# Values and gates of a retention layer as seven half-size products per head in place of eight, with shared sums, in a two-layer trunk on one core

## The chip, the cores and the metric

One Trainium2 chip, one of its cores. The metric is the device time in microseconds of one execution of the program. The engines are called as in the profile: PE does the matmuls (PEld its weight loads), DVE, ACT and POOL do elementwise work, SP issues the loads and stores.

## The reference, cut to what matters

The program is a trunk of two layers over 512 tokens of width 1024. Layer A is a retention layer with 4 heads (keys of 256, values of 512), layer B a latent attention layer with 16 heads. Layer A is what the change touches:

```python
hproj = x @ w_in
qk = H_A * DK_A                                   # 1024
q = hproj[..., :qk].reshape(b, s, H_A, DK_A)
k = hproj[..., qk:2 * qk].reshape(b, s, H_A, DK_A)
v = hproj[..., 2 * qk:2 * qk + WIDTH_A].reshape(b, s, H_A, DV_A)
gate = hproj[..., 2 * qk + WIDTH_A:]
q = _rope(q, ROPE_BASE_A)
k = _rope(k, ROPE_BASE_A) * (DK_A ** -0.5)
o = _chunkwise_retention(q, k, v)                 # decayed causal q k^T v
...
o = ((o - mu) * lax.rsqrt(var + 1e-5)).astype(x.dtype).reshape(b, s, WIDTH_A)
return (o * jax.nn.silu(gate)) @ w_out
...
x = _layer_norm(DEEPNORM_ALPHA * x + y, ln_g[layer], ln_b[layer])
```

For one head, V and the gate are both x (512 x 1024) times a weight of 1024 x 512.

## The kernel before, in words

Every float32 product is made of three matmuls (`mm3`, L84 to L88): each operand is split into a high part, rounded to the format that PE multiplies, and a low part, the rest; high by high, high by low and low by high are summed in PSUM. `split` (L90 to L92) makes the parts: a cast on ACT, then a subtraction on DVE.

The class `Weights` brings the weights in the order of the list `order`: `issue` takes a staging tile (tag `wst`, 2 buffers), starts the load on SP, casts the high part on ACT (L56) and subtracts the low part (L58) on DVE, for every third tile on POOL. `get` keeps two tiles ahead of the one asked for; there are four pairs of high and low parts.

Layer A runs head by head. `proj_qk(h)` makes q and k transposed and applies the rope (L295 to L303) on DVE: two products with an operand in PSUM, a subtraction of two tiles in SBUF, two products, an addition, then the split, for q and for k. `proj_v(h)` and `gate(h)` both call `token_proj` (L309 to L318): four weight tiles, each against four token tiles and two blocks of the contraction, three matmuls of 128x512 each, so 96 a call. Between the two stand the `scores(h)`, which need the rope. `gate` takes tanh on ACT and one operation on DVE. `inner(h)` multiplies the decayed scores by V, one token tile after another, and normalises: statistics (L368, L369) and the argument of the root on DVE, the power on POOL (L202), a product with the gate on DVE (L372), a scaling on ACT (L375). After `inner(h)` comes `out_proj(h - 1)` (96 matmuls into the residual `r`), then `proj_qk(h + 1)`, then `transposes(h)`, 16 transposes of 128x128 and their splits. After the last head, `out_proj(3)` runs token tile by token tile with the layer norm and the transposes of the result.

Layer B begins with the latent projections. The inverse norms of the query latents are four powers on POOL (L202), one per token tile; each lets DVE normalise its tile (L591, L592), which PE then transposes (L242). The rope of the shared key is five operations on POOL (L597 to L601); the rotated key is transposed at L629. `gate_b` (L86 with x1h, then L611 and L613) fills PE ahead of it.

The order on each engine is that of a scheduler, which takes the program's order as priority; each engine's queue is then fixed and runs in order. Loads are issued from SP in program order.

Of the kernel before, what the change touches and what calls it, by code (L numbers as in the profile page):

```python
# [8 lines left out]
F32 = mybir.dt.float32  # L9
# [25 lines left out]
class Weights:  # L35
# [6 lines left out]

    def issue(self, between=None):

        nc = self.nc
        name, aps, n = self.todo.pop(0)
        st = self.stage.tile([P, WC], F32, tag="wst", name="wst")
# [3 lines left out]
        for j, ap in enumerate(aps if isinstance(aps, list) else [aps]):  # L51
# [3 lines left out]
            nc.sync.dma_start(st[:, sl], ap)  # L55
# [15 lines left out]
def trunk_kernel(ctx, tc, a):  # L71
# [106 lines left out]
    zero = keep.tile([P, 512], BF16, tag="kvg", name="zero")  # L178
# [5 lines left out]
    kvg = keep.tile([P, KVL], F32, tag="kvg", name="kvg")  # L184
# [72 lines left out]
    with tc.tile_pool(name="pa", bufs=1) as pa:  # L257
        cosA = pa.tile([P, S], F32, tag="cosA", name="cosA")
        sinA = pa.tile([P, S], F32, tag="sinA", name="sinA")
        decay = pa.tile([P, H_A, S], F32, tag="decay", name="decay")  # L260
# [3 lines left out]
        qk, vv, sT, gs, og, oT = {}, {}, {}, {}, {}, {}  # L264

        def proj_qk(h):
            first = {}
            if h == 0:
                for nm in ("q", "k"):
                    first[nm] = [bank(), bank()]  # L270
                for k in range(KX):
# [5 lines left out]
                    banks = first["q"] + first["k"]  # L277

                    steps = [(i, j) for j in range(3) for i in range(4)] if k == 0 else [(i, j) for i in range(4) for j in range(3)]
                    for i, j in steps:  # L280
                        l, x_ = parts[j]
                        nc.tensor.matmul(banks[i], lhsT=l[:, sls[i]], rhs=x_, start=k == j == 0, stop=k == KX - 1 and j == 2)  # L282
            for nm in ("q", "k"):
                ps = first.get(nm, [])
# [12 lines left out]
                eng = nc.vector
                eng.tensor_tensor(out=rr[:, 0, :], in0=ta, in1=tb, op=ALU.subtract)
                tc_ = pa.tile([P, S], F32, tag="ropeA", name="ropeA")
                td = pa.tile([P, S], F32, tag="ropeB", name="ropeB")  # L300
# [617 lines left out]
```

## Time and profile before

| | |
|---|---|
| median of 3 runs | 947.59 us (947.55 to 949.78) |
| the profiled execution | 947.91 us, span 946.1 us |
| mean granted clock of PE | 0.995 of full |
| busy share of the span | PE 99%, DVE 57%, ACT 35%, POOL 15% |
| layer A, layer B | to about 430 us, from there |

The page gives the busy time of each engine over the span, and the chain of work that ended last. As the engines run side by side, only time on that chain counts: work on DVE, ACT or POOL matters where PE waits for it. A wait shows as the time in brackets behind a row of the timeline, with what ended it, and summed in the view of waits.

### The profile page before, as it was taken

To read this page: it belongs to the slowest core of one execution; us is meant where nothing else is said; L and a number is where in the kernel's file an instruction comes from. 1 tells how busy PE (TensorE), PEld (TensorE's weight loads), DVE (VectorE), ACT (ScalarE), POOL (GpSimd) and SP (SyncE) were. 2 spreads that over 40 slices of the span, in tenths; PEclk is the share of its full clock that TensorE was granted. 3 is DMA by queue.
4 is the path that set the end of the run, shared out by engine and by line. 5 is a ranking of instruction groups with operands and counts; after the bars stand their busy time and mean duration, and the time that the engine had idled before them with its cause. 6 is when DMAs were issued, how large, how long until landed. Compare 5 with 4: busy or idle time off the path is not lost.

```text
span 946.1 us, 11987 instructions
## 1 busy us (share of the span) xinstructions
PE 933.2 (99%) x4649; PEld 792.9 (84%) x4649; DVE 538.9 (57%) x1015; ACT 333.7 (35%) x576; POOL 144.1 (15%) x99
## 2 busy tenths in 40 slices
PE   9999999999999999999989999999999999999996
PEld 6888888888888888888968888888888888888885
DVE  5745545363535435853365667474664737647567
ACT  5333333233323333223433443343343334333431
POOL 0112111111121123012211101001011021111104
PEclk9999999999999999999999999999999999999998
DMA  8832222222212324113224323342233422424222
GB/s 263 294 115 68 89 90 67 89 89 89 89 63 94 106 73 156 45 37 123 62 93 118 113 68 96 105 115 75 78 103 99 111 68 90 117 78 112 90 65 91
DMA packets 31497, 94.30 MB, mean 100 GB/s; under 512 B 4176, under 2 KB 4816, under 8 KB 31440
## 3 DMA queue, kind: packets, MB, share of 16 engines
q1 hardware_dynamic: 27936, 83.96, 27.9%
q10 hardware_dynamic: 3504, 9.57, 4.1%
q8 instruction: 36, 0.59, 0.3%
q14 instruction: 21, 0.17, 0.1%
HBM read 83.03 MB, written 2.10 MB: 90 GB/s over the span
## 4 chain that ended last, share of the span: by engine, by line
PE 93%; issue 3%; DVE 2%; POOL 1%; ACT 0%; DVEq 0%; POOLq 0%; ACTq 0%
PE ps L88 28%; PE ps L87 28%; PE ps L86 28%; PE ps L282 2%; PE ps L678 2%; PE ps L655 1%; PE ps L656 1%; PE ps L386 1%; PE ps L242 1%; PE ps L182 0%; POOL ln_rs L202 0%; POOL rs L202 0%; DVE r L729 0%; POOL wlo L58 0%; DVE wlo L58 0%
## 5 line engine op out<-in xcount | busy, mean ns | idle before, releaser
L56 ACT CAST whi<-wst 128x1024 fp32r<-128x1024 f32 (+3 forms) x159 | 151.4, 953 | 306.5 <-PE ps L88 148.7
L58 POOL TENSOR_TENSOR wlo<-wst,whi 128x1024 fp32r<-128x1024 f32 (+3 forms) x49 | 109.8, 2241 | 682.5 <-ACT whi L56 657.6
L58 DVE TENSOR_TENSOR wlo<-wst,whi 128x1024 fp32r<-128x1024 f32 (+3 forms) x110 | 121.8, 1109 | 150.1 <-ACT whi L56 149.6
L86 PE MATMUL ps<-whi,xTh 128*128 128x512 f32 x256 | 100.1, 391 | 0.0
L87 PE MATMUL ps<-wlo,xTh 128*128 128x512 f32 x256 | 99.6, 389 | 0.0
L88 PE MATMUL ps<-whi,xTl 128*128 128x512 f32 x256 | 99.6, 389 | 0.0
L86 PE MATMUL ps<-qlt_h,whi 128*128 128x512 f32 x144 | 56.9, 395 | 0.0
L663 ACT ACTIVATE p<-ps,sm 128x512 f32<-128x512 f32 (+1 forms) x64 | 33.4, 526 | 66.6 <-DVE sm L660 66.6
L87 PE MATMUL ps<-qlt_l,whi 128*128 128x512 f32 x144 | 56.5, 392 | 0.0
L88 PEld LDWEIGHTS ps<-whi,xTl 128*128 128x128 f32 x256 | 48.1, 188 | 10.0
L88 PE MATMUL ps<-qlt_h,wlo 128*128 128x512 f32 x144 | 56.4, 391 | 0.0
L87 PEld LDWEIGHTS ps<-wlo,xTh 128*128 128x128 f32 x256 | 48.1, 188 | 9.7
L86 PEld LDWEIGHTS ps<-whi,xTh 128*128 128x128 f32 x256 | 48.1, 188 | 9.7
L86 PE MATMUL ps<-x1h,whi 128*128 128x512 f32 x128 | 50.6, 396 | 0.0
L86 PE MATMUL ps<-whi,oTh 128*128 128x512 f32 x128 | 50.0, 391 | 0.0
L87 PE MATMUL ps<-x1l,whi 128*128 128x512 f32 x128 | 50.0, 390 | 0.0
L88 PE MATMUL ps<-x1h,wlo 128*128 128x512 f32 x128 | 49.9, 390 | 0.0
L87 PE MATMUL ps<-wlo,oTh 128*128 128x512 f32 x128 | 49.8, 389 | 0.0
L88 PE MATMUL ps<-whi,oTl 128*128 128x512 f32 x128 | 49.6, 390 | 0.0
L86 PE MATMUL ps<-whi,ogh 128*128 128x512 f32 (+1 forms) x114 | 44.7, 392 | 0.0
L88 PE MATMUL ps<-whi,ogl 128*128 128x512 f32 (+1 forms) x114 | 44.1, 387 | 0.0
L87 PE MATMUL ps<-wlo,ogh 128*128 128x512 f32 (+1 forms) x114 | 44.0, 386 | 0.0
(202 smaller groups left out, 2111.2 us busy)
## 6 DMA issues: line engine op xcount, KB each, us to landing
wst<-in_w_v SPq DMA_DIRECT2D x16, 512.0 KB, 3.3
wst<-in_w_g SPq DMA_DIRECT2D x16, 512.0 KB, 3.3
wst<-in_w_ao SPq DMA_DIRECT2D x16, 512.0 KB, 3.3
wst<-in_w_gb SPq DMA_DIRECT2D x16, 512.0 KB, 3.8
qr<-uv ACTq DMA_DIRECT2D x64, 128.0 KB, 2.4
wst<-in_w_bo SPq DMA_DIRECT2D x16, 512.0 KB, 3.7
wst<-in_w_qk SPq DMA_DIRECT2D x12, 512.0 KB, 3.3
wst<-in_w_q SPq DMA_DIRECT2D x16, 384.0 KB, 3.1
```

What stands on the lines that cost most here:

```text
L56: nc.scalar.copy(hi[:, sl], st[:, sl])
L58: eng.tensor_tensor(out=lo[:, sl], in0=st[:, sl], in1=hi.bitcast(F32)[:, sl], op=ALU.subtract)
L86: nc.tensor.matmul(ps, lhsT=lh, rhs=rh, start=start, stop=False)
L87: nc.tensor.matmul(ps, lhsT=lh, rhs=rl, start=False, stop=False)
L88: nc.tensor.matmul(ps, lhsT=ll, rhs=rh, start=False, stop=stop)
L242: nc.tensor.transpose(out=ps[:, k * P : (k + 1) * P], in_=src[:, k * P : (k + 1) * P], identity=ident)
L282: nc.tensor.matmul(banks[i], lhsT=l[:, sls[i]], rhs=x_, start=k == j == 0, stop=k == KX - 1 and j == 2)
L386: nc.tensor.transpose(out=ps[:, k * P : (k + 1) * P], in_=og[h][:, n, k * P : (k + 1) * P], identity=ident)
L655: nc.tensor.matmul(ps, lhsT=rh[:, qs], rhs=krp[:, :n], start=False, stop=False)
L656: nc.tensor.matmul(ps, lhsT=rl[:, qs], rhs=krp[:, :n], start=False, stop=True)
L663: nc.scalar.activation(pp, ps, AF.Exp, bias=sm[:, qb, 1:2], scale=SCALE_B, accum_out=sm[:, qb, 2:3])
L678: nc.tensor.transpose(out=ps[:, do : do + P], in_=pr[i][:, so : so + P], identity=ident)
```

## The change

With x in four quarters (token halves by halves of the contraction) and the joined weights V|G in four quarters (halves of the contraction by V and gate), the two projections are one 2 x 2 block product. The change computes it with seven products of quarters (`product`, 24 matmuls each) in place of eight, by the scheme of Strassen with shared sums:

- `x_forms` makes four sums of quarters of x once, on POOL, and splits each on ACT and DVE (128x1024).
- `w_vg` brings the four weight quarters of a head, two tiles of 128x1024 each, and makes four sums of quarters: those of `p6` on DVE, those of `p5` and `p7` on POOL, two tiles each. Fourteen weight tiles a head are then split, where there were eight. The first `W.load` of a tile is done in the function that stands in the list; the others reuse what lies in the staging tiles. One quarter is loaded twice.
- `values_and_gates` runs P1, P6, the scores, P2, P5, P7, P4, P3, and adds the products up from PSUM on DVE (`plus`, 14 a head), with two copies on ACT. V is then split, and the gate taken, from tiles in SBUF.
- Staging tiles of layer A: eight in place of two. Layer B has its own two. Tiles share tags in other ways (rope with the scores' parts, q and k with v, the products' sums with the transposed output); the decay is loaded per head; norm weights are loaded later.
- `out_proj(h)` follows `transposes(h)` for heads 0 to 2. Head 3's transposes follow `inner(3)` at once.
- In layer B two of the rope operations on POOL are kept in program order, and the scheduler's order on POOL comes out another way.

The diff, cut to its core:

```diff
+    def w_vg(h):
+        v, g, s = a["w_v"], a["w_g"], {}
+
+        def sub(out, x, y, eng):
+            eng.tensor_tensor(out=out, in0=x, in1=y, op=ALU.subtract)
+            return out
+
+        def p1(t):
+            s["v0", t] = W.load(v[4 * h + t])
+            return s["v0", t]
+
+        def p6(t):
+            s["g0", t] = W.load(g[4 * h + t])
+            s["g1", t] = W.load(g[4 * h + 2 + t])
+            sub(s["v0", t], s["g0", t], s["v0", t], nc.vector)
+            return sub(s["g1", t], s["g1", t], s["v0", t], nc.vector)
+
+        def p2(t):
+            s["v1", t] = W.load(v[4 * h + 2 + t])
+            return s["v1", t]
+
+        def p5(t):
+            sub(s["v1", t], s["v1", t], s["g1", t], nc.gpsimd)
+            return s["v0", t]
+
+        def p7(t):
+            s["g1", t] = W.load(g[4 * h + 2 + t])
+            return sub(s["g0", t], s["g1", t], s["g0", t], nc.gpsimd)
...
     for h in range(H_A):
-        order += w_a("w_v", "v", h) + w_a("w_g", "g", h)
-        if h:
-            order += w_a("w_ao", "o", h - 1)
+        order += w_vg(h)
         if h + 1 < H_A:
             order += [(f"qk{h + 1}", a["w_qk"][4 * h + t], 1024) for t in range(4)]
-    order += w_a("w_ao", "o", H_A - 1)
+        order += w_a("w_ao", "o", h)
...
+        def x_forms():
+            a11, a12 = xv[:, 0:4, 0:256], xv[:, 4:8, 0:256]
+            a21, a22 = xv[:, 0:4, 256:512], xv[:, 4:8, 256:512]
+            f1, f2, f3 = (wst.tile([P, 4, 256], F32, tag="wst", name="xsum") for _ in range(3))
+            nc.gpsimd.tensor_tensor(out=f1, in0=a21, in1=a22, op=ALU.add)
+            nc.gpsimd.tensor_tensor(out=f2, in0=f1, in1=a11, op=ALU.subtract)
+            split(*forms["s2"], f2)
+            nc.gpsimd.tensor_tensor(out=f3, in0=a11, in1=a21, op=ALU.subtract)
+            split(*forms["s3"], f3)
+            split(*forms["s1"], f1)
+            nc.gpsimd.tensor_tensor(out=f2, in0=a12, in1=f2, op=ALU.subtract)
+            split(*forms["s4"], f2)
...
+        def product(name, x_):
+            ps = [bank(), bank()]
+            for t in range(2):
+                wh, wl = W.get(name)
+                for n in range(2):
+                    for j in range(2):
+                        k = 2 * t + j
+                        sl = slice(j * 512, (j + 1) * 512)
+                        mm3(ps[n], x_(k, n), (wh[:, sl], wl[:, sl]), k == 0, k == 3)
+            return ps
+
+        def values_and_gates(h):
...
+            ps1 = product(f"p1.{h}", block(0, 0))
+            for n in range(2):
+                nc.scalar.copy(m[:, 0, n, :], ps1[n])
+            ps6 = product(f"p6.{h}", form("s2"))
+            for n in range(2):
+                plus(m[:, 1, n, :], m[:, 0, n, :], ps6[n])
+            scores(h)
+            ps2 = product(f"p2.{h}", block(4, 0))
...
+            for n in range(2):
+                split(hi[:, n, :], lo[:, n, :], plus(tmp("v"), m[:, 0, n, :], ps2[n]))
+            ps5 = product(f"p5.{h}", form("s1"))
+            for n in range(2):
+                plus(c[:, n, :], m[:, 1, n, :], ps5[n])
+            ps7 = product(f"p7.{h}", form("s3"))
+            for n in range(2):
+                plus(m[:, 0, n, :], m[:, 1, n, :], ps7[n])
+                gated(2 + n, plus(c[:, 2 + n, :], m[:, 0, n, :], ps5[n]))
+            ps4 = product(f"p4.{h}", block(4, 2))
+            for n in range(2):
+                split(hi[:, 2 + n, :], lo[:, 2 + n, :], plus(tmp("v"), m[:, 0, n, :], ps4[n]))
+            ps3 = product(f"p3.{h}", form("s4"))
+            for n in range(2):
+                gated(n, plus(c[:, n, :], c[:, n, :], ps3[n]))
...
         proj_qk(0)
+        x_forms()
         for h in range(H_A):
-            proj_v(h)
...
-            scores(h)
-            gate(h)
+            values_and_gates(h)
...
             inner(h)
-            if h:
-                for half in range(2):
-                    w = [W.get(f"o{h - 1}") for _ in range(2)]
-                    for n in range(NT):
-                        out_proj(h - 1, half, n, w)
             if h + 1 < H_A:
                 proj_qk(h + 1)
             transposes(h)
+            if h + 1 < H_A:
+                for half in range(2):
+                    w = [W.get(f"o{h}") for _ in range(2)]
+                    for n in range(NT):
+                        out_proj(h, half, n, w)
...
-        nc.gpsimd.tensor_tensor(out=ta, in0=raw, in1=cosB, op=ALU.mult)
-        nc.gpsimd.tensor_tensor(out=tb[:, :, 0:32], in0=raw[:, :, 32:64], in1=sinB[:, :, 0:32], op=ALU.mult)
+        tc.keep_in_program_order(nc.gpsimd.tensor_tensor(out=ta, in0=raw, in1=cosB, op=ALU.mult))
+        tc.keep_in_program_order(
+            nc.gpsimd.tensor_tensor(out=tb[:, :, 0:32], in0=raw[:, :, 32:64], in1=sinB[:, :, 0:32], op=ALU.mult)
+        )
```

The order on three queues, in rows of the instruction lists of the two kernels (line, operation, output <- inputs, shape). The first place is DVE after the last split of x, from there to the rope of head 0. Before (`wlo` at L58 are the low parts of weights):

```order
L92 TENSOR_TENSOR xTl<-r,xTh 128x512
L58 TENSOR_TENSOR wlo<-wst,whi 128x512
L58 TENSOR_TENSOR wlo<-wst,whi 128x1024 x2
L295 TENSOR_TENSOR ropeA<-ps,cosA 128x512
L296 TENSOR_TENSOR ropeB<-ps,sinA 128x512
L58 TENSOR_TENSOR wlo<-wst,whi 128x1024
L298 TENSOR_TENSOR rope<-ropeA,ropeB 128x512
```

And now (L65 makes low parts of weights, L100 is `split`, L115 a sum of weights):

```order
L100 TENSOR_TENSOR xTl<-r,xTh 128x512
L65 TENSOR_TENSOR wlo<-wst,whi 128x512
L100 TENSOR_TENSOR s1l<-xsum,s1h 128x1024
L65 TENSOR_TENSOR wlo<-wst,whi 128x1024
L100 TENSOR_TENSOR s2l<-xsum,s2h 128x1024
L65 TENSOR_TENSOR wlo<-wst,whi 128x1024
L100 TENSOR_TENSOR s3l<-xsum,s3h 128x1024
L100 TENSOR_TENSOR s4l<-xsum,s4h 128x1024
L378 TENSOR_TENSOR ropeA<-ps,cosA 128x512
L379 TENSOR_TENSOR ropeB<-ps,sinA 128x512
L382 TENSOR_TENSOR ropeA<-ps,cosA 128x512
L380 TENSOR_TENSOR rope<-ropeA,ropeB 128x512
```

The four forms of x stand ahead of the rope; further down the same queue, the first low part for P6 (the L65 row here) stands behind a sum of weights and most of the rope:

```order
L115 TENSOR_TENSOR wst<-wst 128x1024
L379 TENSOR_TENSOR ropeB<-ps,sinA 128x512
L100 TENSOR_TENSOR qkl<-rope,qkh 128x1024
L380 TENSOR_TENSOR rope<-ropeA,ropeB 128x512
L382 TENSOR_TENSOR ropeA<-ps,cosA 128x512
L383 TENSOR_TENSOR ropeB<-ps,sinA 128x512
L65 TENSOR_TENSOR wlo<-wst,whi 128x1024
L384 TENSOR_TENSOR rope<-ropeA,ropeB 128x512
```

The second place is PE around the end of head 3, before, at the end of `inner(3)`:

```order
L86 MATMUL ps<-vh,sTh 128x512
L87 MATMUL ps<-vl,sTh 128x512
L88 MATMUL ps<-vh,sTl 128x512
L86 MATMUL ps<-whi,oTh 128x512
L87 MATMUL ps<-wlo,oTh 128x512
```

Here the last matmuls of `inner(3)` are followed by the 96 of `out_proj(2)`, and the transposes come after them. Now:

```order
L94 MATMUL ps<-vh,sTh 128x512
L95 MATMUL ps<-vl,sTh 128x512
L96 MATMUL ps<-vh,sTl 128x512
L494 MATMUL ps<-ident,gs 128x128 x16
L94 MATMUL ps<-whi,oTh 128x512
```

The 16 transposes follow `inner(3)` with nothing between. The third place is POOL in layer B, before:

```order
L202 TENSOR_TENSOR rs<-rs_t,mhalf 128x1 x3
L597 TENSOR_TENSOR rbA<-krt,cosB 128x256
L598 TENSOR_TENSOR rbB<-krt,sinB 128x4x32
L599 TENSOR_TENSOR rbB<-krt,sinB 128x4x32
L601 TENSOR_TENSOR krt<-rbA,rbB 128x4x64 x2
L202 TENSOR_TENSOR rs<-rs_t,mhalf 128x1
```

And now:

```order
L250 TENSOR_TENSOR rs<-rs_t,mhalf 128x1 x3
L711 TENSOR_TENSOR rbB<-krt,sinB 128x4x32
L250 TENSOR_TENSOR rs<-rs_t,mhalf 128x1
L707 TENSOR_TENSOR rbA<-krt,cosB 128x256
L709 TENSOR_TENSOR rbB<-krt,sinB 128x4x32
L713 TENSOR_TENSOR krt<-rbA,rbB 128x4x64 x2
```

The fourth power moved from behind the rope of the key to behind its first product.

## Rows read from the trace of the kernel before

**Rows 1.** The page's busy line: us, share of the span, instructions.

```profile
PE 933.2 (99%) x4649; PEld 792.9 (84%) x4649; DVE 538.9 (57%) x1015; ACT 333.7 (35%) x576; POOL 144.1 (15%) x99
```

**Rows 2.** Windows: length, busy PE, PEld, DVE, ACT, POOL; clock, DMA, GB/s.

```profile
103.00:203.00 100.00, 100.00 (x461) 83.47 (x459) 46.96 (x70) 30.46 (x39) 14.19 (x9) 1.00 0.27 87
...
464.00:485.00 21.00, 17.48 (x89) 14.62 (x89) 13.63 (x30) 9.74 (x26) 8.34 (x11) 0.92 0.19 63
```

**Rows 3.** Waits of PE: what for; us in total, times, longest.

```profile
PE ps L242 <- DVE qn L592: 1.6, 1, 1.6
PE ps L242 <- DVE gsb L613: 1.6, 1, 1.6
```

**Rows 4.** Timeline of PE: start, us, line, output<-inputs [wait <-releaser].

```profile
126.60 0.39 PE L86 MATMUL ps<-qh,kh 128*128 128x512 f32 x1
...
130.35 0.45 PE L86 MATMUL ps<-whi,xTh 128*128 128x512 f32 x1
...
466.45 0.39 PE L86 MATMUL ps<-x1h,whi 128*128 128x512 f32 x1
...
471.69 0.39 PE L88 MATMUL ps<-x1h,wlo 128*128 128x512 f32 x1
```

**Rows 5.** Timeline of DVE: head 0, head 3's norm, start of layer B.

```profile
34.50 0.69 DVE L303 TENSOR_TENSOR rope<-ropeA,ropeB 128x512 f32<-128x512 f32 x1
...
35.83 0.68 DVE L296 TENSOR_TENSOR ropeB<-ps,sinA 128x512 f32<-128x512 f32 x1
36.43 1.22 DVE L92 TENSOR_TENSOR ql<-rope,qh 128x1024 fp32r<-128x1024 f32 x1
37.56 2.88 DVE L298 TENSOR_TENSOR rope<-ropeA,ropeB 128x512 f32<-128x512 f32 x1
...
51.57 0.56 DVE L341 TENSOR_TENSOR sf<-ps,decay 128x384 f32<-128x384 f32 x1 [0.37 <-PE ps L88]
52.04 2.74 DVE L92 TENSOR_TENSOR sTl<-sf,sTh 128x512 fp32r<-128x512 f32 x2
...
351.90 0.70 DVE L368 BATCH_NORM_STATS2 o_st<-ps 128x6 f32<-128x512 f32 x1 [0.34 <-PE ps L88]
...
470.80 0.14 DVE L201 TENSOR_SCALAR rs_t<-ss 128x1 f32<-128x1 f32 x1
...
474.40 0.48 DVE L591 SCALAR_TENSOR_TENSOR qn<-ps,rs,qg 128x256 f32<-128x256 f32 x1 [2.78 <-POOL rs L202]
```

**Rows 6.** Timeline of POOL at the same places.

```profile
37.31 2.58 POOL L58 TENSOR_TENSOR wlo<-wst,whi 128x1024 fp32r<-128x1024 f32 x1 [36.00 <-ACT whi L56]
51.36 2.40 POOL L58 TENSOR_TENSOR wlo<-wst,whi 128x1024 fp32r<-128x1024 f32 x1 [11.47 <-ACT whi L56]
...
352.40 2.41 POOL L58 TENSOR_TENSOR wlo<-wst,whi 128x1024 fp32r<-128x1024 f32 x1 [13.88 <-ACT whi L56]
354.77 1.57 POOL L202 TENSOR_TENSOR o_rs<-rs_t,mhalf 128x1 f32<-128x1 f32 x1
...
469.38 0.99 POOL L202 TENSOR_TENSOR rs<-rs_t,mhalf 128x1 f32<-128x1 f32 x1 [0.66 <-DVE rs_t L201]
...
471.04 0.91 POOL L598 TENSOR_TENSOR rbB<-krt,sinB 128x128 f32<-128x128 f32 x1
...
473.82 0.54 POOL L202 TENSOR_TENSOR rs<-rs_t,mhalf 128x1 f32<-128x1 f32 x1
```

**Rows 7.** Timeline of ACT: last tile of x; head 3's first scaling.

```profile
16.41 0.62 ACT L91 CAST xTh<-r 128x512 fp32r<-128x512 f32 x1 [0.75 <-DMA r<-in_xT]
...
356.38 0.72 ACT L375 ACTIVATE og<-og,o_rs 128x512 f32<-128x512 f32 x1 [2.67 <-POOL o_rs L202]
```

**Rows 8.** The chain that ended last: start, us, what.

```profile
5.13 22.21 PE ps L282 x96
...
379.74 1.75 PE ps L386 x16
```

More of the change, by code (lines that the diff above doesn't have):

```diff
@@ L41, in __init__, with load @@
         self.todo, self.ready, self.n, self.place = [], [], 0, {}
+    def load(self, ap):
+        st = self.stage.tile([P, WC], F32, tag="wst", name="wst")
+        self.nc.sync.dma_start(st, ap)
+        return st
     def issue(self, between=None):
@@ L46, in issue @@
         name, aps, n = self.todo.pop(0)
-        st = self.stage.tile([P, WC], F32, tag="wst", name="wst")
+        st = aps() if callable(aps) else self.stage.tile([P, WC], F32, tag="wst", name="wst")
         pool, th, tl = self.place[name].pop(0) if self.place.get(name) else (self.parts, "whi", "wlo")
@@ L176, in trunk_kernel @@
     nc.scalar.copy(warm, mhalf)
-    zero = keep.tile([P, 512], BF16, tag="kvg", name="zero")
+    zero = wst.tile([P, 512], BF16, tag="wst", name="zero")
     nc.vector.memset(zero, 0.0)
@@ L281, in proj_qk @@
                         l, x_ = parts[j]
-                        nc.tensor.matmul(banks[i], lhsT=l[:, sls[i]], rhs=x_, start=k == j == 0, stop=k == KX - 1 and j == 2)
-            for nm in ("q", "k"):
-                ps = first.get(nm, [])
+                        nc.tensor.matmul(four[i], lhsT=l[:, sls[i]], rhs=x_, start=k == j == 0, stop=k == KX - 1 and j == 2)
+            hi = pa.tile([P, 4, S], F32R, tag="bh", name="qkh")
+            lo = pa.tile([P, 4, S], F32R, tag="bl", name="qkl")
+            for w, nm in enumerate(("q", "k")):
+                ps = banks.get(nm, [])
                 for t in range(0 if ps else 2):
@@ L296, in proj_qk @@
                 nc.vector.tensor_tensor(out=tb, in0=ps[1], in1=sinA, op=ALU.mult)
[L297 to L300, printed above, removed]
+                nc.vector.tensor_tensor(out=rr[:, 0:S], in0=ta, in1=tb, op=ALU.subtract)
+                tc_, td = tmp("ropeA"), tmp("ropeB")
                 nc.vector.tensor_tensor(out=tc_, in0=ps[1], in1=cosA, op=ALU.mult)
@@ L320, in proj_v @@
-        def proj_v(h):
-            ps = token_proj(f"v{h}")
-            hi = pa.tile([P, NT, DV_A], F32R, tag="vh", name="vh")
-            lo = pa.tile([P, NT, DV_A], F32R, tag="vl", name="vl")
-            for n in range(NT):
-                split(hi[:, n, :], lo[:, n, :], ps[n])
-            vv[h] = (hi, lo)
+                nc.vector.tensor_tensor(out=rr[:, S : 2 * S], in0=tc_, in1=td, op=ALU.add)
+                split(
+                    hi[:, 2 * w : 2 * w + 2, :].rearrange("p a b -> p (a b)"),
+                    lo[:, 2 * w : 2 * w + 2, :].rearrange("p a b -> p (a b)"),
+                    rr[:, 0 : 2 * S],
+                )
@@ L349, in gate @@
+        def values_and_gates(h):
+            m = pa.tile([P, 2, 2, S], F32, tag="oTh", name="m")
+            c = pa.tile([P, 4, S], F32, tag="oTl", name="c")
             g = pa.tile([P, NT, DV_A], F32, tag="gs", name="gs")
-            for n in range(NT):
-                th = pa.tile([P, DV_A], F32, tag="th", name="th")
-                nc.scalar.activation(th, ps[n], AF.Tanh, scale=0.5)
-                nc.vector.scalar_tensor_tensor(out=g[:, n, :], in0=th, scalar=1.0, in1=ps[n], op0=ALU.add, op1=ALU.mult)
@@ L358, in inner @@
             vh, vl = vv[h]
-            o = pa.tile([P, NT, DV_A], F32, tag="og", name="og")
+            o = gs[h]
             for n in range(NT):
@@ L442, in trunk_kernel @@
                 x1_transposes(n - 2)
+    layer_a.close()
+    W.stage = ctx.enter_context(tc.tile_pool(name="wstB", bufs=2))
     pb = ctx.enter_context(tc.tile_pool(name="pb", bufs=1))
+    kvg = pb.tile([P, KVL], F32, tag="kvg", name="kvg")
+    qg = pb.tile([P, QL], F32, tag="qg", name="qg")
+    nc.sync.dma_start(kvg, a["kv_norm"].broadcast_to([P, KVL]))
+    nc.sync.dma_start(qg, a["q_norm"].broadcast_to([P, QL]))
     lat_h = pb.tile([P, 4, S], F32R, tag="lat_h", name="lat_h")
```

116 lines of the change are left out of this document (63 added, 53 removed).

## The prediction

> **What bounds the kernel now.** I read the page's busy line first: PE is busy 933.2 of a span of 946.1 us, DVE 57% of it, POOL 15% [rows 1]. The windows say where the rest lies: in a stretch of layer A, 103 to 203 us, PE is busy all 100 us at full clock, with DVE at 47 and POOL at 14; from 464 to 485 us PE has 17.48 of 21 us at a granted clock of 0.92 [rows 2]. The waits of PE name that hole: two of 1.6 us, both in layer B's start [rows 3]. So in layer A PE alone sets the time, and all else runs under it. The reader is to see two things: a matmul taken out of layer A is worth its full pitch as long as DVE, ACT and POOL still deliver in time, and the change gives these engines much more to do.
>
> **What is removed.** V and gate of a head are 2 x 96 matmuls of 128x512; seven products of 24 make 168. Over four heads 96 matmuls go. 24 matmuls of this shape start from 466.45 to 471.69, a pitch of (471.69 - 466.45)/23 = 0.228 us [rows 4]. **-21.9 us.** The profiled execution took 947.91 (0.3 above the median 947.59, so the sum is made on 947.91 and 0.3 taken off at the end).
>
> **What is added, and the port.** Four sums of x and up to four weight sums of a head go to POOL, four more to DVE, and the low parts of fourteen weight tiles in place of eight. A pass over 128x1024 takes 1.22 on DVE (1.13 from start to start) and 2.40 on POOL; a 512 pass takes 0.69, from PSUM 0.60 from start to start [rows 5, 6]. These can't run side by side: the rope subtraction at 37.56, both operands in SBUF, took 2.88 us in place of 0.69, and ended 0.55 after the POOL pass that began at 37.31; at 52.04 two low parts of 512 took 2.74 during the POOL pass from 51.36, while the product with an operand in PSUM (51.57, 128x384) ran through it in 0.56 [rows 5, 6]. So a DVE pass with two SBUF operands and a POOL pass exclude each other, and a waiting POOL pass gets in between two DVE passes (the rope subtraction was next in line at 37.56 and POOL went first). One POOL pass thus holds DVE's two-SBUF passes for about 2.3 us.
>
> The Trainium skill, "SBUF — State Buffer", section "Who interferes with whom", gives the rule: DVE and GpSimd share one port pair as an exclusive lock, a DVE instruction with two SBUF inputs contends with a GpSimd instruction that reads SBUF, and whoever issues first blocks the other fully. The trace agrees (2.88 against 0.69); the rule speaks against putting this change's sums on POOL. Read by issue order alone, with DVE's next pass always ahead of a waiting POOL pass, head 0 below would lose some 6 us less; the row at 37.56 speaks for taking turns, and I go by it.
>
> **Head 0: the lag.** Before, the rope of head 0 ran under proj_v(0). Now DVE's order has six passes for the forms of x and the first weights ahead of the rope, and the low part of P6's first weight behind it, while PE has only P1 (24 matmuls, 5.5 us) to do.
> - The last tile of x is cast at 16.41 now [rows 7]; with eight staging buffers its load is not held back, so I take 15.3. From there four POOL passes (9.2) and on DVE two 512 and six 1024 passes (2 x 0.69 + 6 x 1.13 = 8.2) take turns: the last form is done at about 32.7.
> - Then 15 DVE passes up to P6's weight: eight rope products from PSUM (4.8), three rope passes in SBUF (2.1), four of 1024 (4.5): 44.1. qk0 ends on PE at 5.13 + 22.21 = 27.3 [rows 8], P1 at 32.8. **PE idles 11.3.**
> - PE then does half of P6 (2.7) and the scores (126.60 to 130.35: 3.75 [rows 4]), the other half from about 51, when the second weight's low part is through; P2 ends at 59.3. Before P5's first low part DVE has about 4 us of two-SBUF passes, and two POOL low parts and three sums (11.5) get in between: 66.5. **PE idles another 6.7**, some of it perhaps less, as two of those sums wait for loads.
> - A hole lowers the clock: 464 to 485 shows 0.92 of full, that is (1 - 0.92) x 21 = 1.7 us lost beside two waits of 1.6 [rows 2, 3] (half clock, 1.2 in place of 2.4 GHz, for some 3.4 us). For the two holes here together 2.
>
> Sum of head 0: 11.3 + 6.7 + 2 = **+20**. From below: with no exclusion POOL has the forms at 15.3 + 9.6, DVE follows to 27 and the rope to 38.4, so PE idles 5.6 once: 6. From above: x no earlier than 16.41 and 2.58 for each of the nine POOL passes [rows 6] gives 24.
>
> **Heads 1 to 3.** Rope, low parts and forms lie under the 22 us of proj_qk and the 22 of out_proj now. Between P1 and P3 PE has 168 x 0.228 + 3.75 = 42 us; the port must carry 9 POOL passes (20.7) and on DVE 13 passes of 1024 (14.7) and 13 to 14 of 512 and less (9): 44.4. Eight staging buffers and two weights ahead let part of it start earlier. I take 0.5 a head, **+1.5**; the bounds are 0 and, if nothing can be moved out of the stage, 2.4 a head and about 1 for the clock, 10.
>
> **End of layer A.** Before, out_proj(2), 22 us, lay between inner(3) and transposes(3); now the transposes follow at once. For the first token tile it took from the statistics at 351.90 to the end of the scaling at 357.10, 5.2 us, with one POOL pass in the way of the power (1.57 at 354.77 in place of 0.54) [rows 5, 6, 7]. The fourth tile's chain starts when inner(3) ends, and PE has only twelve transposes meanwhile (three quarters of 1.75 = 1.3 [rows 8]): 3.9, and 2.9 without the POOL pass. A weight's low part sits in DVE's row ahead of the fourth tile's (+1.1: 5.0 from above). I take 4, and 1 for the clock: **+5** (2.9 to 6.7). The transposes of heads 0 to 2 follow proj_qk as before: nothing.
>
> **Layer B.** PE, DVE and ACT keep their order; POOL takes the fourth power after one short rope product in place of five operations. Its input was there at 470.94 and it began at 473.82; the last query tile was normalised 0.6 later, at 474.40 [rows 5, 6]. Now it can begin at about 471.3, after the third power (469.38 + 0.99) and that product (0.91 in the row of 471.04): 2.5 earlier. The first wait of 1.6 goes, and the second, on work queued behind it on DVE, shrinks; next late is the rotated key, whose four passes now follow, still ahead of its use. **-2.7** with some of the clock; bounds 0 and 3.2 + 1.7 = -4.9.
>
> Smaller loads, the tags shared between tiles and the later loads of norms are waited for by nobody within some 20 us of PE work: 0.
>
> **Sum.** 947.9 - 21.9 + 20 + 1.5 + 5 - 2.7 = 949.8; less 0.3 for the median: **949.5**.
>
> **Rivals.**
> - *All side work stays hidden.* Then only -21.9 and -2.7 count: 923 to 926. For it speaks the busy line (DVE 57%, POOL 15%); against it that head 0 has no PE work to hide behind. Chance 0.03. The Trainium skill, "Perfetto Trace Analysis", section "Identifying the Most-Contended Engine", says to improve the engine with the highest occupancy first, which here is PE: by it this is the outcome.
> - *The exclusion costs little in this order.* DVE's passes are not split by POOL's; head 0 loses its lower bound, 6, to 10, the end 3 to 5: 947.6 - 21.9 + 8 + 4 - 2.7 = 935. Chance 0.08.
> - *Taking turns, but shorter.* POOL's sums for P5 and P7 come late enough (they wait for loads) not to stand before P5's low part: the second hole and its clock go, head 0 is 12 to 14, the rest as in the sum: 942. Chance 0.19. It decides if the second hole is below 2.
> - *Slower: the port binds heads 1 to 3 as well.* Each later head's stage is 44.4 us of port time against 42 of PE, and low parts come after PE wants them, in P7 and P4 first: 5 to 10 for 1.5, so 953 to 958. It decides when the port time moved out of the stage is under 2 us a head. For it: DVE is in order, and one pass held by POOL holds all behind it. Against: two weights of lead. Chance 0.25.
> - My sum, 945 to 953: 0.45.
>
> **How the numbers follow.** About 0.3% (2.8 us) is what a measurement of this kernel can tell from no change: 944.8 to 950.4. Faster: 0.03 + 0.08 + 0.17 of the short case = 0.28. Same: 0.02 of it and 0.28 of my sum = 0.30. Slower: 0.17 of my sum and 0.25 = 0.42. The range leaves out the first two cases (0.11) and about 0.05 above: 937 to 959. The likeliest case's own range is 945 to 953.
>
> **What would show it.** In the new profile: PE matmuls down by 96; one wait of PE of about 11 us on a low part before P6 of head 0 and one of 5 to 8 before P5; rows of the rope, forms or sums on DVE of 2.5 to 3.5 in place of 0.69 or 1.2, each beside a POOL row; one wait of 3 to 5 on the scaled gate ahead of the last transposes of layer A, with the clock below 1 behind these; the two waits of 1.6 in layer B smaller. I am wrong if PE's waits in head 0 sum to under 14 or over 24, if heads 1 to 3 wait by more than 4, or if the end of layer A waits less than 2.

## The result, and the profile after

The changed kernel takes 958.78 us (957.60 to 958.99, 4 runs) against 947.88 of the kernel before beside it: ratio 1.0106, 95% interval 1.0093 to 1.0120, so slower by some 10.1 us (10.9 between these medians). The forecast was 949.5 in a range of 937 to 959, slower with 0.42 its likeliest outcome: the direction held, the range only just, by 0.2 us; the size was 9 us short, and 945 to 953, the range of the likeliest case, missed the result by 5.8. The profiled execution took 958.76, its span 957.0.

The page's busy line of the changed kernel, against [rows 1]:

```profile
PE 921.5 (96%) x4553; PEld 780.1 (82%) x4553; DVE 657.7 (69%) x1107; ACT 365.9 (38%) x612; POOL 222.0 (23%) x127
```

The 96 matmuls are gone (4553 for 4649), yet PE's busy time fell by 11.7 only, and its idle time grew from 12.9 to 35.5. The waits of PE (what for; us in total, times, longest) say where, against [rows 3]:

```profile
PE ps L95 <- DVE wlo L65: 9.0, 3, 6.3
PE ps L94 <- ACT whi L63: 7.9, 1, 7.9
PE ps L494 <- ACT gs L486: 4.9, 4, 1.7
PE ps L290 <- DVE gsb L725: 1.9, 1, 1.9
PE ps L96 <- DVE oTl L100: 1.9, 1, 1.9
```

The first two lines are head 0, the third the end of head 3, the fourth layer B, the fifth the start of out_proj(1). To turn waits into lost time, take the same landmarks in both chains: the transposes of heads 0, 1 and 2 and the first transposes behind the layer norm. Before:

```profile
103.24 1.75 PE ps L386 x16
202.66 1.75 PE ps L386 x16
302.08 1.75 PE ps L386 x16
...
398.17 0.87 PE ps L242 x8
```

The same in the chain of the changed kernel; those of head 1 are not on its chain and stand at 215.26 in PE's timeline (the second fence). The timeline starts such a group 0.16 earlier than the chain: heads 0 and 2 stand at 121.05 and 313.05 there.

```profile
121.22 1.75 PE ps L494 x16
313.21 1.75 PE ps L494 x16
...
411.98 0.87 PE ps L290 x8
```

```profile
215.26 1.91 PE L494 MATMUL ps<-ident,gs 128*128 128x128 f32 x16
...
219.98 0.55 PE L96 MATMUL ps<-whi,oTl 128*128 128x512 f32 x1 [1.88 <-DVE oTl L100]
```

The low part that this last row waits for stood behind a rope pass on DVE, which took as long as the POOL pass beside it:

```profile
216.66 2.66 DVE L380 TENSOR_TENSOR rope<-ropeA,ropeB 128x512 f32<-128x512 f32 x1
```

```profile
216.40 2.38 POOL L65 TENSOR_TENSOR wlo<-wst,whi 128x1024 fp32r<-128x1024 f32 x1 [13.96 <-ACT whi L63]
```

Each stretch holds 24 matmuls less, 5.5 us by [rows 4]. Head 0, up to its transposes: +18.0, so 23.4 lost. To those of head 1, by the timeline: 94.2 for 99.4, 0.3 lost. To those of head 2: 97.8 for 99.4, 3.8 lost. From there past the end of head 3: 98.8 for 96.1, 8.2 lost. Behind that, layer B: 545.0 for 547.9, 2.9 gained. Together 35.7 - 21.9 - 2.9 = 10.9, the difference of the spans.

What the waits alone don't show is the clock. Windows of the changed kernel (length, busy PE, PEld, DVE, ACT, POOL; clock, DMA, GB/s) around the holes:

```profile
44.00:51.00 7.00, 7.00 (x20) 5.66 (x21) 4.26 (x5) 3.98 (x4) 0.85 (x1) 0.60 0.00 0
...
68.00:75.00 7.00, 6.50 (x18) 5.20 (x19) 5.31 (x8) 3.24 (x4) 0.17 (x1) 0.61 0.63 202
215.00:226.00 11.00, 9.12 (x41) 7.21 (x40) 9.29 (x11) 4.04 (x6) 2.38 (x1) 0.84 0.20 72
226.00:313.00 87.00, 87.00 (x392) 72.44 (x392) 63.95 (x79) 32.74 (x40) 32.60 (x15) 1.00 0.31 101
...
391.00:400.00 9.00, 7.48 (x25) 6.13 (x25) 5.95 (x8) 4.14 (x6) 0.55 (x1) 0.62 0.51 175
...
490.00:498.00 8.00, 7.51 (x35) 6.14 (x36) 5.61 (x12) 2.49 (x4) 2.55 (x2) 1.00 0.29 92
```

Behind the holes of layer A PE runs at half clock for a while: (1 - 0.60) x 7 = 2.8 us lost behind the wait ahead of P6, (1 - 0.61) x 7 = 2.7 behind P5's wait, (1 - 0.84) x 11 = 1.8 behind the wait on oTl, (1 - 0.62) x 9 = 3.4 at the end of layer A. Behind layer B's wait of 1.9 the clock stays at 1.00 (the last row). From 226 to 313, on the way to the transposes of head 2, PE doesn't wait at all.

DVE of the changed kernel in head 0 (timeline: start, us, what, idle before):

```profile
15.78 2.83 DVE L100 TENSOR_TENSOR xTl<-r,xTh 128x512 fp32r<-128x512 f32 x1
18.53 2.89 DVE L65 TENSOR_TENSOR wlo<-wst,whi 128x512 fp32r<-128x512 f32 x1
21.34 3.42 DVE L100 TENSOR_TENSOR s1l<-xsum,s1h 128x1024 fp32r<-128x1024 f32 x1
...
28.10 3.41 DVE L100 TENSOR_TENSOR s3l<-xsum,s3h 128x1024 fp32r<-128x1024 f32 x1
...
42.69 1.22 DVE L65 TENSOR_TENSOR wlo<-wst,whi 128x1024 fp32r<-128x1024 f32 x1
...
50.73 0.69 DVE L405 TENSOR_TENSOR sf<-ps,c 128x512 f32<-128x512 f32 x1 [2.74 <-PE ps L96]
...
57.50 2.50 DVE L100 TENSOR_TENSOR sTl<-sf,sTh 128x512 fp32r<-128x512 f32 x1
59.92 0.68 DVE L432 TENSOR_TENSOR m<-m,ps 128x512 f32<-128x512 f32 x1
60.52 4.64 DVE L100 TENSOR_TENSOR sTl<-sf,sTh 128x384 fp32r<-128x384 f32 x2
...
65.28 3.17 DVE L65 TENSOR_TENSOR wlo<-wst,whi 128x1024 fp32r<-128x1024 f32 x1
```

And POOL beside it:

```profile
15.27 2.79 POOL L333 TENSOR_TENSOR xsum<-r 128x1024 f32<-128x1024 f32 x1 [13.96 <-DMA cosA<-in_cosA]
...
57.05 2.40 POOL L115 TENSOR_TENSOR wst<-wst 128x1024 f32<-128x1024 f32 x1 [1.16 <-DVE wlo L65]
59.41 2.85 POOL L65 TENSOR_TENSOR wlo<-wst,whi 128x1024 fp32r<-128x1024 f32 x1
62.21 5.14 POOL L115 TENSOR_TENSOR wst<-wst 128x1024 f32<-128x1024 f32 x2
```

Passes that took 0.69 in [rows 5] take 2.5 to 2.9 here, each for as long as a POOL pass beside it, while `m`, with an operand in PSUM, takes its 0.68. The four rows held up to 31.5 are together 8.7 us longer than such passes alone, and DVE has no pause of its own from 9.7 to 48.0. P6's low part is ready at 43.9 (forecast 44.1), P5's (the row at 65.28) at 68.4 (forecast 66.5). Ahead of P5's go ten POOL passes: four sums of x, two low parts and four sums of weights (the row at 62.21 holds two).

### The profile page after: what moved, and what is told of

Same layout as the page of the kernel before. It is cut to its first block, busy times and chain, and to the rows that moved or that the text cites. A ratio compares the mean times of both kernels' runs of the same rounds, so it can differ in the third digit from the quotient of the medians.

```text
span 957.0 us, 12030 instructions
## 1 busy us (share of the span) xinstructions
PE 921.5 (96%) x4553; PEld 780.1 (82%) x4553; DVE 657.7 (69%) x1107; ACT 365.9 (38%) x612; POOL 222.0 (23%) x127
## 4 chain that ended last, share of the span: by engine, by line
PE 86%; DVE 8%; issue 2%; DMA 2%; POOL 1%; ACT 1%; SPq 0%; DVEq 0%; POOLq 0%; ACTq 0%
PE ps L95 27%; PE ps L96 27%; PE ps L94 27%; DVE wlo L65 2%; PE ps L790 2%; DMA r<-in_xT 1%; PE ps L767 1%; PE ps L768 1%; DVE sTl L100 1%; DMA g<-in_ln_g 1%; PE ps L290 1%; PE ps L494 0%; DVE rope L380 0%; DVE gs L438 0%; DVE vl L100 0%
## 5 line engine op out<-in xcount | busy, mean ns | idle before, releaser
L63 ACT CAST whi<-wst 128x1024 fp32r<-128x1024 f32 (+3 forms) x183 | 176.1, 965 | 257.8 <-PE ps L96 115.2
L65 POOL TENSOR_TENSOR wlo<-wst,whi 128x1024 fp32r<-128x1024 f32 (+3 forms) x57 | 131.6, 2308 | 602.3 <-ACT whi L63 571.8
L65 DVE TENSOR_TENSOR wlo<-wst,whi 128x1024 fp32r<-128x1024 f32 (+3 forms) x126 | 157.4, 1251 | 83.2 <-ACT whi L63 82.8
L94 PE MATMUL ps<-whi,oTh 128*128 128x512 f32 x128 | 52.0, 406 | 0.0
L115 POOL TENSOR_TENSOR wst<-wst 128x1024 f32<-128x1024 f32 x16 | 44.4, 2790 | 8.2 <-DVE wlo L65 8.0
L96 PE MATMUL ps<-whi,ogl 128*128 128x512 f32 (+1 forms) x114 | 44.1, 387 | 0.0
L841 DVE TENSOR_TENSOR r<-r,ps 128x512 f32<-128x512 f32 (+1 forms) x49 | 32.3, 670 | 10.3 <-PE ps L96 10.2
L94 PE MATMUL ps<-whi,xTh 128*128 128x512 f32 x96 | 37.6, 392 | 0.0
L96 PE MATMUL ps<-xTh,wlo 128*128 128x512 f32 x96 | 37.4, 389 | 0.0
L95 PE MATMUL ps<-wlo,xTh 128*128 128x512 f32 x96 | 37.3, 389 | 0.0
L94 PE MATMUL ps<-xTh,whi 128*128 128x512 f32 x96 | 37.3, 389 | 0.0
```

Of the source, the lines that this page charges most:

```text
L63: nc.scalar.copy(hi[:, sl], st[:, sl])
L65: eng.tensor_tensor(out=lo[:, sl], in0=st[:, sl], in1=hi.bitcast(F32)[:, sl], op=ALU.subtract)
L94: nc.tensor.matmul(ps, lhsT=lh, rhs=rh, start=start, stop=False)
L95: nc.tensor.matmul(ps, lhsT=lh, rhs=rl, start=False, stop=False)
L96: nc.tensor.matmul(ps, lhsT=ll, rhs=rh, start=False, stop=stop)
L115: eng.tensor_tensor(out=out, in0=x, in1=y, op=ALU.subtract)
```

## The experiments

Ratios are to the kernel before on the same chip; "changed" is the changed kernel, 1.0106.

**The four sums of x on DVE.**

```diff
 def x_forms():
-    nc.gpsimd.tensor_tensor(out=f1, in0=a21, in1=a22, op=ALU.add)
+    nc.vector.tensor_tensor(out=f1, in0=a21, in1=a22, op=ALU.add)
...
```

> Changed kernel (958.8), with the four sums of x on DVE in place of POOL, nothing else. Theory 1, the port: in head 0 a POOL pass holds DVE's two-SBUF passes for 2.3 us, so four passes of 1.13 on DVE replace 9.2 us; the scheduler then also puts the second weight of P6 right behind the first. P6 of head 0 starts at about 44 as before, but runs through; P5 starts near 58 in place of 68.5, the second hole (6.3) and the clock behind it go: about 946 (944 to 950). Theory 2, DVE's own queue is too long there whoever else runs: four passes more on DVE make it worse: 961 to 964.

Measured: 947.59, ratio 0.9998 (0.9988 to 1.0007), 10.2 less than changed. More work on DVE made the kernel faster by 1.1%: theory 2 falls. Its waits of PE in head 0:

```profile
PE ps L94 <- ACT whi L63: 10.3, 1, 10.3
```

The hole ahead of P6 stays, as expected, and the one ahead of P5 is gone. The transposes of head 0 start 9.9 earlier (111.28). Two things mix in: the scheduler placed P6's two low parts next to each other, which the expectation counted in, and P5's first low part ahead of the scores, which it did not; that part is made at 50.05 here and at 65.28 in the changed kernel:

```profile
50.05 1.98 DVE L65 TENSOR_TENSOR wlo<-wst,whi 128x1024 fp32r<-128x1024 f32 x1 [1.36 <-ACT whi L63]
```

So this run doesn't tell how much of the 10.2 is the port and how much this order.

**Nothing elementwise of layer A on POOL.**

```diff
-            sub(s["v1", t], s["v1", t], s["g1", t], nc.gpsimd)
+            sub(s["v1", t], s["v1", t], s["g1", t], nc.vector)
...
-            eng = nc.gpsimd if self.n % 3 == 2 and self.n > EAGER else nc.vector
+            eng = nc.gpsimd if self.n % 3 == 2 and self.n > 87 else nc.vector
```

> The same, and also the weight sums for P5 and P7 and all low parts of weights of layer A on DVE: POOL does only the powers there. Theory 1, the port: as with the sums of x alone, and the wait on oTl ahead of out_proj(1) (1.9 and its clock, 4 together) and about 2 of the wait at the end of layer A go, since no POOL pass stands in DVE's way: about 940 (936 to 945); no DVE row of a rope or low part over 1.5 us is left in layer A. Theory 2: DVE gets some 12 us more work a head of 94 and PE waits for it in heads 1 to 3: 958 or more.

Measured: 943.48, ratio 0.9953 (0.9936 to 0.9970). A window over heads 1 and 2:

```profile
105.00:300.00 195.00, 195.00 (x895) 162.23 (x894) 153.10 (x209) 76.84 (x95) 4.39 (x8) 1.00 0.31 104
```

DVE is busy 153 of 195 us, PE all of them: the wait on oTl and its slow matmuls are gone, theory 2 falls again. It is 3.5 above the expected 940, inside its range: the end of layer A still waits 3.7 on the scaled gate, and head 0 still 10.2 ahead of P6. By the same landmarks 20 of the 35.7 us are still lost with no sum and no low part on POOL: 13.2 in head 0 (its transposes start at 110.93) and 6.8 at the end. P5's first low part stands ahead of the scores here too (51.99).

**P2 ahead of P6.**

```diff
-        return [entry(f, t) for f in (p1, p6, p2, p5, p7, p4, p3) for t in range(2)]
+        return [entry(f, t) for f in (p1, p2, p6, p5, p7, p4, p3) for t in range(2)]
...
+            ps2 = product(f"p2.{h}", block(4, 0))
             ps6 = product(f"p6.{h}", form("s2"))
```

> Changed kernel, with P2 ahead of P6 in every head (products and weights in the order P1, P2, P6, P5, P7, P4, P3; V's first half is still split behind the scores); POOL keeps its work. P2 needs no sum of x and no sum of weights. If the loss of head 0 is one of order (PE reaches a product that needs sums before they exist, with 5.5 us of P2 left undone): P5 starts near 59 in place of 68.5: about 947 (944 to 951). If DVE and POOL simply can't do the work ahead of P5 sooner, whatever the order: P5 stays near 68, 957 to 960.

Measured: 952.44, ratio 1.0045 (1.0030 to 1.0060): 5.8 less than changed, between the two. Its waits:

```profile
PE ps L95 <- POOL wlo L65: 5.4, 1, 5.4
...
PE ps L95 <- DVE wlo L65: 3.4, 1, 3.4
PE ps L94 <- ACT whi L63: 3.2, 1, 3.2
```

P2 fills part of the first hole: PE's waits in head 0 sum to 12.0 for 16.9, about the 5.5 us of P2 less. But as the ninth weight P6's first low part now falls to POOL, PE waits for that, and P5 starts at 66.0 and not near 59. So the order counts; that POOL is late by the port (a sum of weights ahead of that low part, at 46.27, took 5.49 in place of 2.40) is read from the row and not tested by itself.

**Discarded matmuls in both holes of head 0.**

```diff
+            fill(42 if h == 0 else 0)
             ps6 = product(f"p6.{h}", form("s2"))
...
+            fill(22 if h == 0 else 0)
             ps5 = product(f"p5.{h}", form("s1"))
```

> Changed kernel, with 42 discarded matmuls of 128x512 (parts of x, result never read) behind P1 of head 0 and 22 ahead of P5 of head 0, 9.6 and 5.0 us at full clock, inside the two holes of 11 and 6.3. If part of the loss is the clock that falls behind a hole (matmuls 0.43 us apart in place of 0.23 for some 5 us behind each): the clock stays at 1.00, about 3.5 to 6 less: 953 to 955.5. If the slow matmuls have another cause, or DVE alone sets the end of head 0: 958 to 960.

Measured: 956.92, ratio 1.0090 (1.0075 to 1.0105). This time tells nothing of what the clock costs: the scheduler saw another PE and put P5's first low part (the second of the two passes in this row) before the scores on DVE, so that the second hole would have closed by itself and the 22 matmuls stood in P5's way (64.3 to 69.4):

```profile
51.58 6.00 DVE L65 TENSOR_TENSOR wlo<-wst,whi 128x1024 fp32r<-128x1024 f32 x2 [0.67 <-ACT whi L63]
```

It does tell something of the order: POOL keeps all its work in this kernel, and still P5's low part is ready at 57.6, before PE is done with P2 (64.3). So the next kernel filled the second hole only, where the lists of DVE, ACT, POOL and SP stay as they were.

**Discarded matmuls in the second hole alone.**

```diff
+            fill(24 if h == 0 else 0)
             ps5 = product(f"p5.{h}", form("s1"))
```

> Changed kernel (1.0106 of the kernel before), with 24 discarded matmuls of 128x512 (5.5 us at full clock; parts of x, result never read) in front of P5 of head 0, inside the wait of 6.3 us there; all other queues keep their order, which they did not in the run that filled both holes. If the matmuls 0.43 us apart behind that hole (68.5 to 73.4) are the clock's answer to it: P5 starts at 68.5 again, but at 0.23 us a matmul, 2 to 2.4 less, 1.0081 to 1.0086. If they have another cause: 1.0100 to 1.0112.

Measured: 954.97 (952.09 to 955.80, 5 runs), ratio 1.0059 (1.0045 to 1.0074), 4.5 below changed; its profiled execution took 955.80, 3.0 below that of changed. The window behind the hole, against 0.61 above:

```profile
68.00:75.00 7.00, 5.99 (x27) 4.87 (x27) 6.87 (x10) 3.42 (x5) 1.05 (x1) 1.00 0.55 167
```

P5 waits still, until 69.1 (the kernel was 0.5 later from P6 on), but at full clock behind it, and head 0's transposes stand 1.7 earlier (119.53). So the slow matmuls are the clock's answer to PE's idling, worth about 2.2 us here. The rest of the gain is not the work of the discarded matmuls: of the 3.0 between the two traces 1.7 are head 0 and 1.6 the stretch to the transposes of head 2 (the end of layer A is 0.5 longer, layer B 0.2 shorter). There PE waits 1.9 for oTl as in the changed kernel, but in this execution the clock stays at 1.00 behind it, against 0.84 above:

```profile
213.30:224.30 11.00, 9.11 (x49) 7.39 (x47) 9.89 (x12) 4.04 (x6) 2.38 (x1) 1.00 0.21 73
```

It stays at 1.00 behind the same wait in the traces of four other runs (the sums of x, P2 first, both holes, the end of layer A). Behind the waits of 4.8 to 10.3 us in head 0 the clock fell in every trace here.

**Layer B's POOL order alone, on the kernel before.**

```diff
-        nc.gpsimd.tensor_tensor(out=ta, in0=raw, in1=cosB, op=ALU.mult)
+        tc.keep_in_program_order(nc.gpsimd.tensor_tensor(out=ta, in0=raw, in1=cosB, op=ALU.mult))
...
```

> Kernel before (947.9) with nothing of the change but the two rope products on POOL in layer B kept in program order. If the fourth power's place in POOL's queue was what layer B waited for: both waits of 1.6 shrink and the clock holds, 2.9 less as between the two traces behind the first layer norm: 945.0 (944.5 to 945.7). If layer B of the changed kernel is shorter for another reason (its staging, its loads): 947.6 to 948.2.

Measured: 946.18 against 948.84, ratio 0.9969 (0.9956 to 0.9982): 2.9 less by the ratio, 2.7 by the medians. Its wait of PE on the gate in layer B:

```profile
PE ps L242 <- DVE gsb L615: 2.0, 1, 2.0
```

The wait on the last query tile is gone; that on the gate is not. In the profiled execution, the slowest of the five (947.32), layer B is only 1.5 shorter (546.4 for 547.9): the clock fell behind the wait on the gate (0.79 over 8 us), which it did not in the changed kernel. So POOL's order is the source of the gain of layer B; its size, 1.7 to 4.2 by the interval, takes in what the clock does behind that wait.

**Transposes between the halves of the next projections.**

```diff
+                if w and between:
+                    between()
                 ps = banks.get(nm, [])
...
-                proj_qk(h + 1)
-            transposes(h)
+                proj_qk(h + 1, lambda: transposes(h))
+            else:
+                transposes(h)
```

> Changed kernel (958.8) with the transposes of heads 0 to 2 between the q half and the k half of the next head's projections, so that 11 us of PE work lie between them and out_proj. If the wait of 1.9 on oTl ahead of out_proj(1) and the slow matmuls behind it are the 4.0 us that the stretch from the second to the third transposes lost: 954.8 (954 to 955.5). If the loss there is port time of heads 1 to 3 in general, it turns up as another wait: 957 to 959.

Measured: 955.07, ratio 1.0064 (1.0049 to 1.0079), 4.0 less than changed. The wait on oTl is gone and heads 1 and 2 lose nothing (transposes at 110.42, 204.40 and 298.38).

**The end of layer A.**

```diff
+            for f in (last_g, last_v) if h == 3 else (last_v, last_g):
+                f()
...
-            transposes(h)
+            transposes(h, range(NT) if h + 1 < H_A else (0, 1))
...
             out_proj(3, 1, n, w[2:])
+            if n < 2:
+                transposes(3, (n + 2,))
```

> Changed kernel (958.8); in head 3 P3 comes before P4, and the last layer's transposes are taken two ahead, the other two between the tiles of out_proj(3), so that each tile's norm chain lies under matmuls. If the 8.2 us lost at the end of layer A (four waits of together 4.9 on the scaled gate, the rest clock) come from the transposes following inner(3) at once: 6 to 7 of it go: 952 to 953.5. If the chain of the first tiles is itself late (DVE behind by the last sums): half of it stays, 954.5 to 957.

Measured: 954.86, ratio 1.0061 (1.0046 to 1.0076): 4.3 less, about half of the 8.2. This is the second theory's outcome. The four waits of 4.9 became 0.7, and new ones came, of 1.4 on oTh and of 0.4 and 0.2 on V's parts. The clock stays at 1.00 throughout:

```profile
PE ps L94 <- ACT oTh L99: 1.4, 1, 1.4
...
PE ps L504 <- ACT gs L492: 0.7, 1, 0.7
```

```profile
376.00:402.00 26.00, 23.29 (x107) 18.23 (x106) 23.73 (x42) 9.71 (x14) 5.70 (x6) 1.00 0.25 82
```

**Everything together.** The edits of the runs without POOL, with P2 first, with the transposes between the halves, and at the end.

> Everything together: no elementwise work of layer A on POOL, P2 ahead of P6, transposes between the halves of the projections, the end as in the run on the end of layer A. From the run without POOL (943.5): head 0, which there lost 13.2, loses 5 less as P2 fills half of its hole; the end loses 5 of 6.8 less: 933 to 936. If P2's low parts land behind the forms on DVE as its row suggests, only 3 of the 5 come: 936 to 937.5.

Measured: 936.19 against 948.84, ratio 0.9871 (0.9855 to 0.9887), between the two cases. What is left in head 0 is a wait of 5.2 on P2's low part, behind the forms on DVE.

**Sums of x when they are needed.**

```diff
+            if h == 0:
+                x_form_2(g)
             ps1 = product(f"p1.{h}", block(0, 0))
+            if h == 0:
+                x_form_1(g)
...
             ps5 = product(f"p5.{h}", form("s1"))
+            if h == 0:
+                x_form_3(g)
+                x_form_4(g)
...
+                    if within and n == 3 and mb == 2:
+                        within()
```

> The run with everything together (0.987 of the kernel before, 936.2), with the sums of x made when they are needed: those for P6 first, that for P5 behind P1, those for P7 and P3 behind P5 in the program (two of them in the gates' buffer in place of staging tiles), and the first of head 3's transposes inside the last token tile of inner(3). If what was left of head 0 (8.8 us: a wait of 5.2 ahead of P2, 1.0 ahead of P7 and slow matmuls behind them) is DVE doing sums that nobody waits for yet ahead of low parts that PE waits for: P2 starts when P1 ends, 5 to 7 go in head 0 and 1.5 at the end: 928 to 931, 0.979 to 0.982 of before. If DVE simply has too much to do ahead of P6 in any order: the hole moves to P6 and 934 to 937 stay.

Measured: 933.59 against 948.09, ratio 0.9846 (0.9831 to 0.9860): 2.4 less than everything together, with intervals that just touch, and 3 short of what was expected. Of the 5 to 7 expected in head 0 only 0.7 came (its transposes start at 95.64 for 96.38); the end of layer A gave 1.2. Windows of head 0 in it:

```profile
27.30:49.80 22.50, 21.57 (x100) 17.42 (x98) 22.50 (x27) 8.03 (x9) 0.00 (x0) 1.00 0.25 86
49.80:57.60 7.80, 5.69 (x24) 4.43 (x24) 7.80 (x15) 3.92 (x7) 0.00 (x0) 1.00 0.39 131
57.60:66.00 8.40, 7.47 (x20) 5.47 (x21) 8.39 (x9) 4.94 (x6) 0.00 (x0) 0.59 0.56 178
```

P2 and P6 run with less than 1 us of waiting, but DVE is busy without a pause from 27.3 to 66: the hole moved to P7 (2.1 and 0.9), and the clock behind it costs (1 - 0.59) x 8.4 = 3.4. So the second theory is the nearer one, with P7 for P6: in head 0 DVE is now the bound in this order. That no other order of this work does better is not shown.

**Every third low part on POOL again.**

```diff
-            eng = nc.gpsimd if self.n % 3 == 2 and self.n > 87 else nc.vector
+            eng = nc.gpsimd if self.n % 3 == 2 and self.n > EAGER else nc.vector
```

> The same, with every third low part of layer A's weights on POOL again (sums stay on DVE). If a POOL pass costs DVE its full length only where DVE is late, that is in head 0 and at the end of layer A, and is free in between: 1 to 4 slower than the run beside it. If POOL takes load off DVE, as the busy shares would have it: 1 to 3 faster.

Measured: 944.48, ratio 0.9964 (0.9950 to 0.9978), 11 slower than the run beside it. Heads 1 and 2 lose nothing (94.0 each). Of the 9.7 between the two traces 7.1 are head 0 (its transposes start at 102.73 for 95.64), where one wait stands out; 1.7 are layer B, where the clock fell behind the wait on the gate:

```profile
PE ps L95 <- POOL wlo L65: 9.3, 1, 9.3
```

POOL's first pass there, P6's low part, took 10.7 us in place of 2.4; the row holds it and the next one, and DVE's rows beside it follow:

```profile
38.83 12.98 POOL L65 TENSOR_TENSOR wlo<-wst,whi 128x1024 fp32r<-128x1024 f32 x2 [37.52 <-ACT whi L63]
```

```profile
38.13 2.35 DVE L115 TENSOR_TENSOR wst<-wst 128x1024 f32<-128x1024 f32 x2
40.40 1.22 DVE L100 TENSOR_TENSOR qkl<-rope,qkh 128x1024 fp32r<-128x1024 f32 x1
...
44.94 2.35 DVE L65 TENSOR_TENSOR wlo<-wst,whi 128x1024 fp32r<-128x1024 f32 x2
55.38 0.69 DVE L419 TENSOR_TENSOR sf<-ps,c 128x512 f32<-128x512 f32 x1 [8.09 <-PE ps L96]
```

POOL finished 2.2 us after DVE's queue ran dry at 47.3.

## Why the prediction was right, and where it was short

- **What is removed**, -21.9: right. Where PE doesn't wait a head is 5.4 shorter.
- **The port**: right in what it does to DVE's rows, with the size that was counted (each held pass some 2.2 longer). As the cause of the whole loss it is not shown. With the POOL work of layer A on DVE, the time falls by 1.5% (1.0106 to 0.9953) though DVE has more to do; but 20 of the 35.7 us lost remain, and P5's first low part moved ahead of the scores along with it, which by the run with both holes filled closes the second hole while POOL keeps its work. The two were not separated. The Trainium skill, "SBUF — State Buffer", section "Who interferes with whom", has the exclusive lock that these rows show (2.5 to 2.9 us for a pass of 0.69); on who goes first see the last section.
- **Head 0**, +20, measured 23.4. P6's low part came at 43.9 for 44.1; waits of PE sum to 16.9 for 18.0. Three steps make up the 3.4. The sum itself was 1 short: by its own times the loss up to P5's low part is 66.5 - (27.3 + 3 x 5.5 + 3.75) = 19, not 11.3 + 6.7 = 18. P5's low part was 1.9 later: "two POOL low parts and three sums" were two and four, and the scores came late after the slow matmuls (DVE waited 2.74 for them at 50.73); no run separates these two. And "for the two holes here together 2" was too little: the clock took 2.8 behind the first, which lies within the second wait and shows only in what it made late, and 2.2 to 2.7 behind the second.
- **Heads 1 to 3**, +1.5, measured 4.1: the general port loss that the term was for is next to nothing (0.3 in head 1). But "The transposes of heads 0 to 2 follow proj_qk as before: nothing" failed: out_proj now reads their output at once, and behind the transposes of head 1 a rope pass held by POOL (2.66 in place of 0.69) delayed a low part by 1.9, with 1.8 of clock behind it, together the 4 that moving the transposes brought back. The chain moved past them was costed, the reader behind them was not.
- **End of layer A**, +5, measured 8.2: the mechanism was right, waits 4.9 for 4; the clock was 3.4 for 1.
- **Layer B**, -2.7, measured 2.9, in part by luck. The first wait went as forecast; the second, which was to shrink, is 1.9 for 1.6. What made up for it is the clock, which stayed up behind that wait in this execution; in four traces with the same POOL order it fell there, and layer B took 546.4 to 546.5 for 545.0.

Of its signs of being wrong none came: PE's waits are 16.9 in head 0 (14 to 24), 1.9 in heads 1 to 3 (under 4) and 4.9 at the end (over 2).

Sum: 3.4 + 2.6 + 3.2 - 0.2 account for 9.0 of the 9.3 that were missing; about half of it (0.5, 1.8 and 2.4) is the clock, costed by one hole of layer B [rows 2] in which only eight matmuls ran slow. The rival that the port binds heads 1 to 3 came nearest to the time (953 to 958) by a wrong mechanism. Of the rival that all side work stays hidden, the best kernel here reached 14.5 of 24.6 us: it took the sums off POOL, a product that needs no sums into the first hole, and cover for each chain. The Trainium skill's rule from "Perfetto Trace Analysis", "Identifying the Most-Contended Engine", to improve the busiest engine first, is borne out by that kernel and not by the change as it stood.

## What to carry to other kernels

Before work is put on an engine because it is idle, look in the trace for rows of the neighbour that grow in its presence: a POOL pass here cost DVE its own 2.3 us, so 15% busy was not free time. Price a hole of the bound engine as the wait plus what the windows behind it show at half clock (here 1.8 to 3.4 us in layer A, and nothing in some executions behind a wait of 1.9), and follow late results of the slow stretch into the next queue. When a step is moved, cost not only what it passes but who now reads its result next.

## What was not expected of the hardware

A POOL pass that meets DVE's two-SBUF passes is not always let in between two of them. In the kernel before (37.56) and in the changed one (15.78, 18.53, 21.34) it went ahead of the DVE pass next in line; in the last run above it waited while seven DVE passes that began after it went by, 10.7 us for one pass. What decides between the two was not found. The Trainium skill's section on who interferes with whom says that issue order decides; the first rows agree with that, and the 10.7 us show that passes issued later can go first too. The prediction took turns for granted; for a low part on POOL that PE waits for, the other case is the dearer one.

The clock's answer to the same short wait differs from one execution to the next. Behind the wait of 1.9 on oTl it was 0.84 over 11 us in the changed kernel's trace and 1.00 in five others; behind the wait of 1.9 to 2.0 on layer B's gate 0.79 over 8 us in four traces and 1.00 in eight. What decides was not found. So two traces can lie 1.5 to 1.8 us apart for each such wait, whatever the change between them.
